# Four instead of six deferred tiles in a decoder layer's output projection, with their inputs converted in a fixed order

## The chip, the cores and the metric

The kernel runs on one core of one Trainium2 chip. The metric is the device time of one execution in microseconds (us); three runs of the kernel before gave 1334.19, 1337.36 and 1341.72 us, so the median is 1337.36. The engines are called TensorE (PE in the profile), VectorE (DVE), ScalarE (ACT), GpSimd (POOL) and SyncE (SP), which issues the transfers.

## The reference

One decoder layer is computed for a prompt of 1,024 tokens and for 64 sample tokens (8 sequences of 8), 1,088 tokens in all, with 1,024 features each:

```python
h = rms_norm(x, norm_mix_g)
proj = h @ w_in
a_val, a_gate, q, k, v = jnp.split(proj, [...], axis=-1)
...
a = jax.nn.silu(layer_norm(depthwise_conv_valid(a_full, conv_a_w, conv_a_b), ln_a_g, ln_a_b))
o = attend(q, k, v).reshape(B, S, D_ATTN)
x = x + jnp.concatenate([a, o], axis=-1) @ w_out
h = rms_norm(x, norm_ffn_g)
g_full = jnp.concatenate([ffn_past, h @ w_ffn_gate], axis=1)
g = depthwise_conv_valid(g_full, ffn_conv_w, ffn_conv_b)
x = x + (jax.nn.silu(g) * (h @ w_ffn_up)) @ w_ffn_down
```

The outputs are the normed result, the new keys and values, and the convolutions' states. What the change touches is the product with `w_out`, the residual sum, the norm behind it, and the first tiles of the products with `w_ffn_gate` and `w_ffn_up`.

## The kernel before

Features lie on the 128 partitions and tokens along the free dimension, so `x` is eight tiles of 128 x 1,088. Every fp32 operand of a product is split into a high and a low part (`hi = copy of x` on ScalarE, rounded; `lo = x - hi` on GpSimd or VectorE), and each product is three matmuls: high by high, high by low and low by high.

The product with `w_out` runs over eight feature tiles of the concatenated branch outputs, which are written to DRAM (`mixed`) and read back. It is cut by these input tiles into parts of 3, 3 and 2 (`PARTS`). The first two parts are done by `out_part` (line 855), for each of the eight output tiles in turn: load the weights into a staging buffer (tag WR, two of them), split them into two tiles of tag W (five of them), multiply, and add into `x2[m]`. These products are written so that they fill TensorE while the last heads of attention wait for other engines. The second part (input tiles 3 to 5) is done over all 1,088 tokens only for the output tiles that aren't deferred, in pieces of 384, 384 and 320 tokens (`CHUNKS`). For the deferred ones, `ORDER[:DEFER]`, it is done over the first 544 tokens only, in two pieces of 272 (`HALF`); the rest is left for later.

The last part (input tiles 6 and 7, which attention finishes last) is done by `out_half` (line 1090), once for the first 544 tokens (`out_half(0, ...)`) and once for the others (`out_half(1, ...)`), over the output tiles in the order 4, 5, 6, 7, 0, 1, 2, 3. For each output tile: the products, 12 matmuls of 272 columns in each half; in the second half for a deferred tile 18 more of the second part ahead of them; an addition into the residual on VectorE (L1102), a store of it to DRAM (L1103), a square on ScalarE (L1105), and an addition to the sum of squares on VectorE (L1109). `out_half(1)` also holds the first half's norm: a hook behind output tile j = 1 takes the root (`root`: ten small matmuls at L208, some small steps on VectorE, L210 to L223, and a square root on ScalarE), a hook behind j = 2 spreads it over the partitions (`spread`: transposes at L235 and a copy at L237).

Ahead of `out_half` the inputs are made ready: the last part's inputs (loaded at L975, high parts at L977, low parts at L978 on VectorE) and weights (loads at L983, parts at L988 and L989); the second halves of the three inputs that the deferred products use (L1000 to L1004); their weights, two output tiles to a staging buffer (L1007 to L1014); then four blocks of the first gate weights, `gate0`, and of the first up weights, `up0` (loads at L1035; conversions at L1041, L1042, L1053, L1054; all low parts on GpSimd). None of these conversions is tied to a place in its engine's queue.

Behind `out_half(1)` the first half's normed tiles are scaled and split (`first_blocks`: scaling at L1115, high parts at L1021, low parts at L1022) into the blocks b11 and b21, and `first_half(gate0)` multiplies them. Between its two products stands `between()`, the second half's root; behind the second step of its second product the root is spread. Then the second half's tiles are scaled and split into b22, t1, t3, t2 and t4, and `first_half(up0)` and two `second_half` calls follow. From then on the FFN runs over pairs of feature tiles, `ffn_pair(j)`, which load further weights through the same two staging buffers.

The program's framework sets the order of each engine's queue: it simulates a timeline and takes, of what is ready in it, what comes first in program order. `tc.issue_after(ins)` places what is traced under it behind `ins` in the queue of the engine that `ins` runs on, without a semaphore; instructions of other engines aren't bound by it. On the chip each engine then takes its queue in that fixed order.

## Time and profile before

| what | value |
|---|---|
| median of 3 runs | 1337.36 us (1334.19 to 1341.72) |
| the profiled execution's own time | 1339.12 us |
| its span | 1337.3 us |
| TensorE busy | 1294.3 us, 97% |
| VectorE, ScalarE, GpSimd busy | 930.6, 563.5 and 494.4 us |
| mean granted TensorE clock | 0.988 |

The span is the time from the first to the last record of the profiled execution; its own time, measured from outside, is 1.8 us more. Times inside the span are counted from its start. The stretch that the change edits lies between about 505 us (the last part of attention) and 665 us (the first pair of the FFN). A line of the view of waits says which engine and line waited, for what, for how long in all, how often and the longest time. A line of a timeline gives the start, the duration, the engine and line, the operation with its tiles and shapes, and in brackets the idle time before it with what ended it; rows that follow each other closely are merged (`x2`). Matmuls overlap in their pipeline, so the pace is read from one start to the next, not from a duration.

### The profile page before, as it was taken

Reading aid. Unit: us, or ns where it says so; the run is one execution under the profiler, and the core shown is the slowest. Engines: PE = TensorE matmul, PEld = TensorE weight load, DVE = VectorE, ACT = ScalarE, POOL = GpSimd, SP = SyncE. Lnnn points to the kernel's source line nnn. Section 1 sums busy time; section 2 is a strip of 40 time slices with the busy share of each in tenths; the row PEclk is TensorE's granted clock in tenths of the full one; section 3 lists DMA queues with packets and bytes.
Section 4 is the critical chain, followed back from the end, with each engine's and each line's share of the span. In section 5 each row is a group of like instructions: output and inputs, shape, how many; then the busy total and the mean of one; then the engine's idle time right before and its main releaser. Section 6 shows DMA issues by size and latency. Waiting matters only on the chain.

```text
span 1337.3 us, 26024 instructions
## 1 busy us (share of the span) xinstructions
PE 1294.3 (97%) x10329; PEld 1252.8 (94%) x10329; DVE 930.6 (70%) x1779; ACT 563.5 (42%) x1132; POOL 494.4 (37%) x400
## 2 busy tenths in 40 slices
PE   7999999999999998999999999999999999999996
PEld 7999998999978887889999999999999999999996
DVE  6369779656674656577977677676776659967656
ACT  6412221456674567354534233333333345334432
POOL 1211112111101111870757556464555534444610
PEclk8999999999998999999999999999999999999998
DMA  8147767555779878661023231332313395352412
GB/s 310 56 131 286 281 234 194 181 177 159 219 235 256 218 249 263 201 235 43 14 109 121 92 123 44 111 122 91 119 36 121 101 353 194 108 186 85 156 40 95
DMA packets 94010, 212.30 MB, mean 159 GB/s; under 512 B 13888, under 2 KB 43584, under 8 KB 93888
## 3 DMA queue, kind: packets, MB, share of 16 engines
q1 hardware_dynamic: 93888, 210.64, 48.1%
q8 instruction: 81, 1.33, 0.4%
q14 instruction: 41, 0.34, 0.1%
HBM read 154.56 MB, written 56.04 MB: 157 GB/s over the span
## 4 chain that ended last, share of the span: by engine, by line
PE 81%; DVE 9%; DMA 6%; issue 2%; ACT 1%; POOL 1%; SPq 1%; DVEq 0%; POOLq 0%; ACTq 0%
PE g L186 6%; PE g L188 6%; PE g L187 6%; PE py L925 4%; PE py L927 4%; PE py L928 4%; PE g L925 4%; PE g L928 4%; PE g L927 4%; PE pz L927 3%; PE pz L928 3%; PE pz L925 3%; PE o L746 3%; PE px L925 3%; PE px L928 3%; PE px L927 3%
## 5 line engine op out<-in xcount | busy, mean ns | idle before, releaser
L162 POOL TENSOR_TENSOR wl<-wr,wh 128x1024 fp32r<-128x1024 f32 (+1 forms) x36 | 67.0, 1861 | 278.8 <-PE g L188 152.1
L186 PE MATMUL g<-xh,wh 128*128 128x384 f32 (+1 forms) x472 | 157.5, 334 | 2.5 <-DVE qkv L449 1.4
L188 PE MATMUL g<-xh,wl 128*128 128x384 f32 (+1 forms) x472 | 155.9, 331 | 0.0
L187 PE MATMUL g<-xl,wh 128*128 128x384 f32 (+1 forms) x472 | 155.8, 330 | 0.0
L925 PE MATMUL g<-ux,as 128*128 128x272 f32 x504 | 145.1, 288 | 0.4 <-DVE x L1499 0.4
L928 PE MATMUL g<-ux,as 128*128 128x272 f32 x504 | 145.3, 288 | 0.0
L927 PE MATMUL g<-ux,as 128*128 128x272 f32 x504 | 144.7, 287 | 0.0
L1054 POOL TENSOR_TENSOR wb<-wr,wb 128x512 fp32r<-128x512 f32 x84 | 121.5, 1457 | 51.1 <-ACT wb L1053 51.1
L1409 POOL TENSOR_TENSOR as<-ar,as 128x640 fp32r<-128x640 f32 (+1 forms) x56 | 89.2, 1602 | 104.3 <-ACT as L1408 92.5
L1053 ACT ACTIVATE wb<-wr 128x512 fp32r<-128x512 f32 x84 | 52.5, 628 | 165.4 <-DVE wr L1070 105.1
L925 PEld LDWEIGHTS g<-ux,as 128*128 128x128 f32 x504 | 95.0, 189 | 0.8 <-issue 0.6
L928 PEld LDWEIGHTS g<-ux,as 128*128 128x128 f32 x504 | 94.8, 188 | 0.0
L927 PEld LDWEIGHTS g<-ux,as 128*128 128x128 f32 x504 | 94.7, 188 | 0.0
L186 PEld LDWEIGHTS g<-xh,wh 128*128 128x128 f32 x472 | 89.3, 189 | 4.9 <-issue 2.4
L1279 DVE SCALAR_TENSOR_TENSOR fc<-gb,prm,fc 128x1104 f32<-128x1104 f32 x44 | 82.5, 1893 | 14.7 <-ACT fc L1277 14.4
L698 ACT ACTIVATE y<-y,m 128x128 f32<-128x128 f32 (+1 forms) x192 | 88.5, 464 | 7.4 <-DVE m L686 7.2
L187 PEld LDWEIGHTS g<-xl,wh 128*128 128x128 f32 x472 | 89.3, 189 | 0.1
L188 PEld LDWEIGHTS g<-xh,wl 128*128 128x128 f32 x472 | 89.3, 189 | 0.1
L1054 POOL TENSOR_TENSOR wa<-wr,wa 128x512 fp32r<-128x512 f32 x42 | 58.1, 1386 | 78.2 <-ACT wa L1053 74.2
L160 ACT ACTIVATE wh<-wr 128x1024 fp32r<-128x1024 f32 (+1 forms) x36 | 29.5, 820 | 134.4 <-PE g L188 104.2
L399 DVE SCALAR_TENSOR_TENSOR cacc<-gp,prm,cacc 128x1024 f32<-128x1024 f32 x60 | 84.3, 1405 | 0.1
L661 DVE CUSTOM_DVE_ANT_0 y<-s,pmk 128x128 f32<-128x128 f32 (+1 forms) x192 | 63.8, 377 | 28.0 <-PE s L657 25.4
(381 smaller groups left out, 4315.2 us busy)
## 6 DMA issues: line engine op xcount, KB each, us to landing
cr<-in_kc SPq DMA_DIRECT2D x24, 768.0 KB, 7.8
cr<-in_vc SPq DMA_DIRECT2D x24, 768.0 KB, 7.8
ux<-ub SPq DMA_DIRECT2D x63, 272.0 KB, 4.1
kk<-dk SPq DMA_DIRECT2D x48, 256.0 KB, 5.6
wr<-in_w_gate SPq DMA_DIRECT2D x22, 512.0 KB, 3.3
wr<-in_w_up SPq DMA_DIRECT2D x22, 512.0 KB, 4.6
wr<-in_w_in SPq DMA_DIRECT2D x20, 512.0 KB, 4.8
ub<-u SPq DMA_DIRECT2D x18, 544.0 KB, 3.9
```

The source lines that it names most:

```text
L162: lo_eng.tensor_sub(lo, raw, hi.bitcast(F32))
L186: nc.tensor.matmul(ps[c], whi[:, k, :], xh[:, t0:t0 + n], start=(k == 0), stop=False)
L187: nc.tensor.matmul(ps[c], whi[:, k, :], xl[:, t0:t0 + n], start=False, stop=False)
L188: nc.tensor.matmul(ps[c], wlo[:, k, :], xh[:, t0:t0 + n], start=False, stop=(k == nk - 1))
L399: eng.scalar_tensor_tensor(acc[:, :S], gp[:, j:j + S], col(w0 + j), acc[:, :S], op0=ALU.mult, op1=ALU.add)
L698: nc.scalar.activation(y, y, AF.Exp, bias=m[:, 4 * g + i:4 * g + i + 1], scale=-1.0, accum_out=den[:, g, 2 * hd + u, i:i + 1])
L925: nc.tensor.matmul(ps, whi[:, k, :], xh[:, t], start=(start and k == 0), stop=False, skip_group_check=True)
L927: nc.tensor.matmul(ps, whi[:, k, :], xl[:, t], start=False, stop=False, skip_group_check=True)
L928: nc.tensor.matmul(ps, wlo[:, k, :], xh[:, t], start=False, stop=(stop and k == nk - 1), skip_group_check=True)
L1054: nc.gpsimd.tensor_sub(lo, x, hi.bitcast(F32))
L1279: nc.vector.scalar_tensor_tensor(c[:, :W], gb[i][:, t:t + W], col(C_FW + 3 * f + t), c[:, :W], op0=ALU.mult, op1=ALU.add)
L1409: nc.gpsimd.tensor_sub(lo, raw, hi.bitcast(F32))
```

## The change

`DEFER` goes from 6 to 4: the output tiles 0 and 1 do the second part over all tokens in `out_part`. The loads for the deferred products are chained, each behind the one before on SyncE's queue and all behind the last part's inputs; the three inputs now come ahead of the weights. Their conversions are put in a list of seven (three inputs, four tiles' weights), and `out_half(0)`'s hook issues one of them behind each of the squares j = 1 to 7 on ScalarE; the low parts stay on GpSimd. `gate0`'s loads and conversions and `up0`'s loads are traced behind `out_half(0)` instead of ahead of it. `up0`'s conversions are traced in `between()`, and its low parts go from GpSimd to VectorE, behind the last step of the second half's root.

```diff
@@ -60,7 +60,7 @@
...
-ORDER, DEFER = (4, 5, 6, 7, 0, 1, 2, 3), 6
+ORDER, DEFER = (4, 5, 6, 7, 0, 1, 2, 3), 4
...
@@ -960,7 +960,6 @@
         sft = zt("F", "sft", 1, "sft", NF * B * 2).rearrange("p (j b t) -> p j b t", b=B, t=2)
         early = {"gate": [zt("F", "WA", 2, "wa", D, F32R) for _ in range(2)],
                  "shared": [zt("F", "tmp", 4, "ta", HN) for _ in range(2)],
-                 "wd": [slot("t4", "wh", w=384) for _ in range(4)],
                  "up": [slot("t4", "wa", w=D // 2) for _ in range(4)], "rb": [slot("t3", "rb", F32)],
                  "b21": [slot("b21", "wh", w=512)], "t2": [slot("t2", "mh")], "b11": []}
 
@@ -994,24 +993,40 @@
 
         n1 = PARTS[-2]
         kd = k0 - n1
-        deferred, wd = [], {}
-        for i in range(n1):
-            raw = slot("t2", "mx", F32)
-            nc.sync.dma_start(raw, mixed[kd + i][:, HN:])
+        deferred, wd, later = [], {}, []
+
+        def later_input(raw):
             hi, lo = slot("t3", "mh"), slot("t3", "ml")
             nc.scalar.activation(hi, raw, AF.Copy)
             nc.gpsimd.tensor_sub(lo, raw, hi.bitcast(F32))
             deferred.append((hi, lo))
+
+        def later_weight(m, raw):
+            hi, lo = [slot("b22", t, w=n1 * P) for t in ("wh", "wl")]
+            nc.scalar.activation(hi, raw, AF.Copy)
+            nc.gpsimd.tensor_sub(lo, raw, hi.bitcast(F32))
+            wd[m] = [t.rearrange("p (k c) -> p k c", c=P) for t in (hi, lo)]
+
+        def load_later(dst, src):
+            nonlocal last_load
+            with tc.issue_after(last_load):
+                last_load = nc.sync.dma_start(dst, src).ins
+
+        for i in range(n1):
+            raw = slot("t2", "mx", F32)
+            load_later(raw, mixed[kd + i][:, HN:])
+            later.append((later_input, raw))
         for m0 in ORDER[:DEFER:2]:
             raw = wp.tile([P, D], F32, tag="WR", name=nm("wr"), bufs=WR)[:, :2 * n1 * P]
-            last_load = nc.sync.dma_start(raw.rearrange("p (m c) -> p m c", m=2),
-                                          w_out[m0:m0 + 2, :, kd * P:k0 * P].rearrange("m p c -> p m c")).ins
+            load_later(raw.rearrange("p (m c) -> p m c", m=2),
+                       w_out[m0:m0 + 2, :, kd * P:k0 * P].rearrange("m p c -> p m c"))
             for i in range(2):
-                r = raw[:, i * n1 * P:(i + 1) * n1 * P]
-                hi, lo = [slot("b22", t, w=n1 * P) if len(wd) < 4 else early["wd"].pop(0) for t in ("wh", "wl")]
-                nc.scalar.activation(hi, r, AF.Copy)
-                nc.gpsimd.tensor_sub(lo, r, hi.bitcast(F32))
-                wd[m0 + i] = [t.rearrange("p (k c) -> p k c", c=P) for t in (hi, lo)]
+                later.append((later_weight, m0 + i, raw[:, i * n1 * P:(i + 1) * n1 * P]))
+
+        def convert(j, square):
+            for call, *args in later[j - 1:j] if j else ():
+                with tc.issue_after(square):
+                    call(*args)
...
@@ -1035,15 +1050,15 @@
...
-        def weight_parts(x, new):
+        def weight_parts(x, new, eng):
             n = x.shape[-1]
             hi, lo = new
             nc.scalar.activation(hi, x, AF.Copy)
-            nc.gpsimd.tensor_sub(lo, x, hi.bitcast(F32))
+            eng.tensor_sub(lo, x, hi.bitcast(F32))
             hi, lo = [t.rearrange("p (k c) -> p k c", c=P) for t in (hi, lo)]
             return [(hi[:, i:i + 4], lo[:, i:i + 4]) for i in range(0, n // P, 4)]
 
-        def block_tile(x, zone=False):
+        def block_tile(x, zone=False, eng=nc.gpsimd):
 
             if zone:
                 t = early["gate"].pop(0) if early["gate"] else zt("F", "WA", 2, "wa", D, F32R)
@@ -1051,7 +1066,7 @@
                 t = wp.tile([P, D], F32R, tag="W", name=nm("wb"))
             hi, lo = t[:, :half], t[:, half:]
             nc.scalar.activation(hi, x, AF.Copy)
-            nc.gpsimd.tensor_sub(lo, x, hi.bitcast(F32))
+            eng.tensor_sub(lo, x, hi.bitcast(F32))
...
@@ -1077,12 +1092,6 @@
...
-        gate0 = plain_blocks(weight_raw(w_gate, 0))
-        raw = weight_raw(w_up, 0)
-        up0 = []
-        for i in range(2):
-            up0 += weight_parts(raw[0][:, i * half:i * half + half], early["up"][2 * i:2 * i + 2])
-        up0 += [block_tile(raw[1][:, i * half:i * half + half]) for i in range(2)]
...
@@ -1102,12 +1111,12 @@
                 residuals.append(nc.vector.tensor_add(x, all_of(ps), x).ins)
                 nc.sync.dma_start(x2d[m][:, c], x)
                 s = slot("t1", "sq", F32)
-                nc.scalar.activation(s, x, AF.Square)
+                square = nc.scalar.activation(s, x, AF.Square).ins
                 if j == 0:
                     acc = s
                 else:
                     nc.vector.tensor_add(acc, s, acc)
-                hook(j)
+                hook(j, square)
...
@@ -1117,10 +1126,10 @@
         def new_root(s):
             return early["rb"].pop() if early["rb"] else slot("t3", s, F32)
 
-        sq0, _ = out_half(0, lambda m: None)
+        sq0, _ = out_half(0, convert)
         rs = []
 
-        def norm_first(j):
+        def norm_first(j, square):
             if j == 1:
                 rs.append(root(sq0, D, HN))
             elif j == 2:
@@ -1132,6 +1141,8 @@
                     scale(0, i, rs[0])
                 split(x2[i][:, :HN], tag, i - k)
 
+        gate0 = plain_blocks(weight_raw(w_gate, 0))
+        raw, up0 = weight_raw(w_up, 0), []
         sq1, residuals = out_half(1, norm_first)
         quads = [(*halves(x2[k]), *halves(x2[k + 4])) for k in range(4)]
 
@@ -1159,6 +1170,11 @@
 
         def between():
             rs.append(root(sq1, D, HN))
+            with tc.issue_after(rooted[0]):
+                for i in range(2):
+                    up0.extend(weight_parts(raw[0][:, i * half:i * half + half], early["up"][2 * i:2 * i + 2],
+                                            nc.vector))
+                up0.extend(block_tile(raw[1][:, i * half:i * half + half], eng=nc.vector) for i in range(2))
 
         def spread_second(k, last):
             if k == 1:
```

## The prediction

> **What bounds the kernel now.** I began with the page's head and busy times.
>
> ```profile
> span 1337.3 us, 26024 instructions
> ...
> PE 1294.3 (97%) x10329; PEld 1252.8 (94%) x10329; DVE 930.6 (70%) x1779; ACT 563.5 (42%) x1132; POOL 494.4 (37%) x400
> ```
>
> TensorE is busy 97% of the span; only what delays TensorE, or lets its clock fall, costs time. The view of what TensorE waited for lists few waits, and three of the longer ones lie in the stretch that the change edits: the start of the first half's output products (L977), the first deferred products (L1003) and the first half's norm (the memset L210 stands in VectorE's queue right behind the root's last step, L223).
>
> ```profile
> PE g L925 <- ACT mh L977: 3.2, 1, 3.2
> ...
> PE g L235 <- DVE rv L210: 1.5, 1, 1.5
> ...
> PE g L927 <- POOL ml L1003: 1.2, 3, 0.8
> ...
> PE py L925 <- DVE gb L1260: 0.8, 1, 0.8
> ```
>
> To price them I cut that stretch into windows. The columns are the window, its length, TensorE's busy time with its matmuls in brackets, then the other engines; after POOL stand the granted clock and the DMA share.
>
> ```profile
> 561.30:568.60 7.30, 4.05 (x20) 3.65 (x19) 3.26 (x3) 3.83 (x8) 5.87 (x5) 0.77 0.75 270
> 568.60:578.64 10.04, 10.04 (x83) 10.04 (x81) 6.71 (x10) 6.15 (x12) 7.07 (x7) 1.00 0.73 256
> 578.64:585.30 6.66, 5.06 (x24) 4.09 (x23) 6.56 (x8) 5.05 (x10) 6.66 (x5) 0.75 0.89 345
> ...
> 594.95:596.70 1.75, 0.28 (x3) 0.09 (x2) 1.72 (x4) 0.00 (x0) 1.58 (x2) 1.00 0.88 306
> 596.70:611.80 15.10, 15.10 (x119) 14.89 (x120) 14.22 (x22) 7.18 (x12) 0.00 (x0) 1.00 0.28 97
> ```
>
> ```profile
> 567.27 0.43 PE L928 MATMUL g<-mh,wl 128*128 128x272 f32 x1
> 567.50 0.43 PE L927 MATMUL g<-ml,wh 128*128 128x272 f32 x1
> ...
> 568.72 0.29 PE L928 MATMUL g<-mh,wl 128*128 128x272 f32 x1
> 568.85 0.29 PE L925 MATMUL g<-mh,wh 128*128 128x272 f32 x1
> ```
>
> Starts in the timeline of TensorE give the pace: 0.125 us from one 272-column matmul to the next at full clock (568.72 to 568.85), 0.23 at the lower one (567.27 to 567.50). At full clock, 20 matmuls are 2.5 us, so the first window loses 4.8 of its 7.30 us; the third has 24, or 3.0 us, and loses 3.7 of 6.66; the fourth is 1.75 us in which TensorE has almost nothing, a loss of 1.6. The second, between them, is full, and so is the last, in which VectorE is nearly full too. I call the losses A (4.8), B (3.7) and C (1.6): 10.1 us, the pool from which this change can draw. Two of them hold a slower clock, 0.77 and 0.75, as well as idle time.
>
> **Why they are there.** SyncE's queue, GpSimd and ScalarE:
>
> ```profile
> 556.00 0.33 SPq L766 DMA_DIRECT2D mixed<-cat  x1
> 556.44 2.84 SPq L983 DMA_DIRECT2D wr<-in_w_out  x2
> 559.33 0.50 SPq L975 DMA_DIRECT2D mx<-mixed  x1
> ...
> 567.07 3.97 SPq L1007 DMA_DIRECT2D wr<-in_w_out  x2
> 571.14 1.37 SPq L1000 DMA_DIRECT2D mx<-mixed  x3
> ...
> 594.06 0.33 SPq L1035 DMA_DIRECT2D wr<-in_w_gate  x1
> ```
>
> ```profile
> 557.86 1.01 POOL L162 TENSOR_TENSOR wl<-wr,wh 128x384 fp32r<-128x384 f32 x1 [1.54 <-ACT wh L160]
> ...
> 575.60 2.49 POOL L1013 TENSOR_TENSOR wh<-wr,wh 128x384 fp32r<-128x384 f32 x2 [2.27 <-ACT wh L1012]
> 578.05 5.41 POOL L1003 TENSOR_TENSOR ml<-mx,mh 128x544 fp32r<-128x544 f32 x3
> ...
> 591.01 3.02 POOL L1042 TENSOR_TENSOR wa<-wr,wa 128x512 fp32r<-128x512 f32 x2 [1.11 <-ACT wa L1041]
> 594.02 2.51 POOL L1054 TENSOR_TENSOR wb<-wr,wb 128x512 fp32r<-128x512 f32 x2
> ```
>
> ```profile
> 574.99 0.53 ACT L1012 ACTIVATE wh<-wr 128x384 fp32r<-128x384 f32 x1 [2.78 <-DMA wr<-in_w_out]
> 575.42 0.64 ACT L1105 ACTIVATE sq<-x 128x544 f32<-128x544 f32 x1
> ...
> 643.33 0.64 ACT L1053 ACTIVATE wa<-wr 128x512 fp32r<-128x512 f32 x1 [0.79 <-issue]
> ```
>
> A is latency: attention's last output is stored at 556.00 (L766), the last products' inputs are requested at 559.33 (L975), and the output products that fill TensorE meanwhile run out at 561.3. B is order: the deferred inputs are requested last (L1000, 571.14), behind weight loads (L1007) that wait for staging buffers, and GpSimd makes their low parts (L1003, from 578.05 to 583.5) behind the sixth tile's weights (L1013, 575.60). ScalarE sits 2.78 us at 574.99 on such a weight load, with squares queued behind it.
>
> **The change, part by part.** *Four tiles, not six.* Two tiles' second halves go from out_half(1) back to out_part: 2 x 18 matmuls x 0.125 = 4.5 us of TensorE, only moved (the tile's 1,088 columns, now in three pieces, are the same work). In out_part they lie ahead of A, and so fill it: its end goes from 561.3 to about 565.8. The inputs' first high parts ended the wait 3.2 us after 561.3, at about 564.6, so the gap could close. Two things can undo that. Weight tiles come from five buffers, two to a tile, so the low part of the last weights (L162, 557.86) must then wait for products that end up to 4.5 us later; the two L983 loads wait for staging that this frees, and L975 stood behind them. And attention's own steps may be held up by the added filler. Bounds: 0 (the gap moves along) to 4.8 (gone). I take 3.3, leaving about 0.5 us of idle and 1.0 of slow clock, because L975 comes first in program order and is free to pass a delayed L983.
>
> A rule of the Trainium skill (page TensorE: Matmul & The Clock Gate, Part 1) says that the clock drops after at least one idle window of about 3.4 us. Loss B disagrees: its longest single wait is 0.8 us, and yet the clock was 0.75. By the rule the short gap left in A would cost no slow clock and the sum below would be 7.9, not 6.9; I go by the row.
>
> *The bound order.* The loads become L975, then the three deferred inputs, then two weight loads, each issued after the one before; the seven conversions go one behind each of the squares 1 to 7 of out_half(0). A wait is added on ScalarE: behind a conversion whose load is late stand the later squares, then VectorE's sums of them (L1109) and the root. Say out_half(0) starts at t. A tile is 12 matmuls, 1.5 us; eviction, square and conversion behind it are 0.71, 0.64 and about 0.65.
>
> ```profile
> 580.38 0.71 DVE L1102 TENSOR_TENSOR x<-g,x 128x544 f32<-128x544 f32 x1
> 581.01 1.23 DVE L1109 TENSOR_TENSOR sq<-sq,sq 128x544 f32<-128x544 f32 x1
> ...
> 592.80 1.25 DVE L221 TENSOR_TENSOR rt<-rr 128x5 f32<-128x5 f32 x1
> ...
> 613.81 2.38 DVE L1109 TENSOR_TENSOR sq<-sq,sq 128x544 f32<-128x544 f32 x3
> 619.00 0.16 DVE L212 TENSOR_SCALAR rv<-g 128x4 f32<-128x4 f32 x1 [2.81 <-PE g L208]
> ...
> 619.71 0.17 DVE L221 TENSOR_TENSOR rt<-rr 128x5 f32<-128x5 f32 x1 [0.28 <-ACT rr L218]
> ...
> 624.37 5.66 DVE L1115 SCALAR_TENSOR_TENSOR x<-x,prm,rb 128x544 f32<-128x544 f32 x8 [4.08 <-ACT rb L237]
> ...
> 652.32 0.68 DVE L1068 TENSOR_TENSOR s<-wr 128x512 f32<-128x512 f32 x1
> ```
>
> (0.71 and 1.23 in the first two rows are the eviction L1102 and a sum L1109 while GpSimd runs.) The first input's high part is ready at t + 3.0 + 2.1 = t + 5.1. GpSimd's three low parts at 1.8 each (5.41 for the three of L1003) end at t + 10.6, the first weights' (1.0 to 1.5, from the 2.49 and 2.51 for pairs of L1013) at t + 11.9; the first deferred product is due at t + 12.0, the second weights 3.8 us after that (30 matmuls). It just fits. With sums at 1.23, VectorE takes 1.9 us a tile instead of 1.5 and the chain slips by about half a us. Bounds for what goes of B: 1.0 (the chain slips by 2 us and the clock falls again) to 3.7. I take 3.0.
>
> *Two weight pairs fewer; gate and up weights later.* GpSimd loses L1013's last pair, 2.5 us, and up0's four low parts (L1042 and L1054 from 591.01, 5.5 us). The four of gate0 stay, behind the deferred weights: staging frees at about t + 13.5 and 15.5, a load takes some 3.3 us (3.34 in the chain of waits, for the same size), so they end near t + 23, long before first_half wants them.
>
> ```profile
> 586.94 3.34 DMA wr<-in_w_up
> ```
>
> The root's three steps took 1.25 us each beside up0's GpSimd work and 0.17 with GpSimd idle (L221 at 592.80 and 619.71). After the change the first root starts near t + 20, beside gate0's conversions instead of up0's. Bounds for C: -0.5 to 1.6; I take 0.6, since gate0 still covers most of it.
>
> *up0's low parts on VectorE.* Four subtractions of 128x512 behind the second root, 0.68 each (L1068, the same size, at 652.32): 2.7 us. They land where VectorE sits 4.08 us waiting for the spread root (before 624.37). ScalarE's four high parts aren't bound to that and go into idle time. The loads of pair 1's gate weights (L1035 at 594.06 and after), which wait for the same two staging buffers, move behind those subtractions, some 25 us later; their first conversion (L1053) is only at 643.33, so about 20 us of slack covers it, and a us beyond that would cost a us.
>
> *Less cover.* From the first spread to the first gate products TensorE had 15.1 us of work (the window from 596.70) and will have 10.6. VectorE must in that time scale and split b11 and b21, and finish the eight sums for the second root.
>
> ```profile
> 617.86 1.10 PE L208 MATMUL g<-ones,sq 128*128 128x1 f32 x10
> ```
>
> The sums end at 616.2 (613.81 + 2.38), 1.7 us ahead of the root's matmuls at 617.86. With 4.5 us less in between, TensorE would wait 2.8 us if VectorE kept its order. But sums and evictions are traced ahead of the splits and come ready sooner, and a b21 split isn't needed until a us after the root, the last one 4.5 us later still. In all VectorE gets 4.5 + 2.7 = 7.2 us tighter against idle time of 2.81 + 4.08 = 6.9. Bounds: 0 to 2.8 lost at the root, up to 7.2 if none of that idle time can be used; I take 0.
>
> Sum: 3.3 + 3.0 + 0.6 - 0 = 6.9 us. The profiled execution took 1339.1 us for a span of 1337.3; it becomes 1332.2 (span 1330.4). It lies 1.8 above the median of 1337.4, so the median becomes 1330.5, 0.52% less. All that follows is bound by TensorE and should just start earlier. Half a per cent is about what a measurement of this kernel can tell from no change: 6.7 us, so below 1330.7 is faster and above 1344.1 slower.
>
> **The rivals.** *The gap moves instead of closing.* The five weight buffers hold back L983 and with it L975, or the filler delays attention's last steps, so A stays whole and only B and C pay: 3.6 us, 1333.8. For it: no row shows slack in that chain; the last L162 ends at 558.9 and L983's second load and L975 follow at once. Against: program order puts L975 first.
>
> *VectorE becomes the bound behind out_half(1).* If its two idle stretches are waits that move along with TensorE, they take up nothing: the 7.2 us reappear on TensorE at the second root and at the b22 products, with 1.6 us of slow clock after such a gap (A's 4.8 less the wait of 3.2). That is 8.8 against 6.9 saved: 1.9 slower, 1339.3. It decides from the point where the sums end after TensorE has reached the root. For it: VectorE is 14.22 us busy in the 15.10 us after 596.70, and TensorE already waits 0.8 us for it at L1260. Against: the idle 4.08 is right where the subtractions are put.
>
> *All three losses go whole*, GpSimd being done before the root starts: 10.1 us, 1327.3.
>
> **How the numbers follow.** The forecast has 0.55, two thirds of it below the bound (its centre lies 0.2 below, and A can pay more): 0.37 faster, 0.18 the same. The moved gap 0.20 (0.18 the same, 0.02 slower, should attention's end suffer more than the gap). VectorE as the bound 0.13 (0.08 the same, 0.05 slower, where the slow clock lasts). All three losses whole 0.12, faster. Faster 0.49, same 0.44, slower 0.07. The forecast's own range is 1327.5 to 1334; for eight in ten I go from 1326 (the whole pool and a us of scatter) to 1337.5 (half of the VectorE case left out).
>
> **What would show it.** Right: the window between out_part's end and out_half(0) has less than 1.5 us without matmuls; the wait for L1003's successor on GpSimd is gone and the clock stays at 1.00 there; DMA requests for deferred inputs come before 568; the four subtractions stand on VectorE between the second root and L1115 without a wait of TensorE behind them; first_half starts about 7 us earlier than 611.8. Wrong: TensorE idles as long as before ahead of out_half(0) (the moved gap), waits at the second root or for b22 (VectorE), or ScalarE's conversions hold squares back for a late load.

## The result and the profile after

The changed kernel takes 1345.57 us (median of 9 runs, 1341.79 to 1349.71) against 1336.41 (9 runs, 1333.16 to 1341.72) of the kernel before: a ratio of 1.0067 (95% interval 1.0047 to 1.0086), 9 us slower. The prediction was 1330.5. The profiled execution of the changed kernel took 1341.79, the lowest of its runs.

```profile
span 1340.1 us, 25967 instructions
...
PE 1294.4 (97%) x10311; PEld 1251.1 (93%) x10311; DVE 936.2 (70%) x1785; ACT 561.6 (42%) x1130; POOL 486.6 (36%) x394
```

TensorE's busy time is what it was (1294.3), so no work was added. The span is only 2.8 us longer because attention happened to run shorter: its last product (L746) starts at 542.6 instead of 548.3. (The stretch ahead of it scatters: from the first L657 to the last L746 it took 320.0 us here and 326.4 in e4_gps, a kernel below that is the same up to there.) From that product to the last matmul the changed execution takes 8.1 us more, 789.4 instead of 781.3, which agrees with the medians.

The same kind of windows as in the prediction, now over the changed kernel (window, length, TensorE's busy time with matmuls in brackets, PEld, DVE, ACT, POOL, granted clock, DMA share, GB/s):

```profile
560.08:566.35 6.27, 4.08 (x20) 3.64 (x19) 3.00 (x3) 3.78 (x6) 4.33 (x4) 0.73 0.55 198
...
576.30:583.50 7.20, 5.04 (x24) 4.43 (x23) 4.87 (x5) 3.41 (x7) 7.17 (x6) 0.76 0.94 345
583.50:593.18 9.68, 9.68 (x80) 9.65 (x80) 4.77 (x10) 3.55 (x7) 5.49 (x4) 1.00 0.52 181
593.18:603.76 10.58, 10.58 (x85) 10.37 (x84) 9.46 (x15) 7.30 (x13) 0.00 (x0) 1.00 0.35 129
...
616.30:621.10 4.80, 3.34 (x28) 3.06 (x27) 3.24 (x12) 2.33 (x6) 0.00 (x0) 1.00 0.01 2
```

At 0.125 us a matmul, A (the first row, 20 matmuls) loses 6.27 - 2.5 = 3.8 us; it was 4.8. B (the second, 24) loses 7.20 - 3.0 = 4.2; it was 3.7. C is gone: the third and fourth rows, on both sides of the first root's spread at 593.18, are full. So 1.0 - 0.5 + 1.6 = 2.1 us were saved, of 6.9 foreseen. And there is a new loss in the last row, where TensorE is busy 3.34 of 4.80 us. What TensorE waited for from 540 to 700 us:

```profile
PE py L928 <- POOL wb L1069: 1.8, 1, 1.8
PE g L925 <- ACT mh L976: 1.7, 1, 1.7
PE g L235 <- DVE rr L223: 1.5, 1, 1.5
PE g L925 <- ACT wh L1006: 1.3, 2, 0.9
PE g L928 <- POOL wl L1007: 0.9, 1, 0.9
```

The second, fourth and fifth rows are A and B. The third is the new wait at the second root's spread; the first is one at the second FFN pair, `ffn_pair(1)`, whose gate products take 19.3 us there and took 16.1 before: 3.2 us more. The last new loss lies much later, where the products with `w_ffn_down` begin (L925 with `ux`, behind the last up product `pz`). TensorE's timeline, and VectorE's for the instruction that it waits for:

```profile
1080.73 0.28 PE L928 MATMUL pz<-t4h,wb 128*128 128x272 f32 x1
1084.41 0.36 PE L925 MATMUL g<-ux,as 128*128 128x272 f32 x1 [3.40 <-DVE u L1314]
```

```profile
1083.55 0.72 DVE L1314 TENSOR_TENSOR u<-pz,u 128x544 f32<-128x544 f32 x1
```

The kernel before has no wait there (`pz` at 1083.53 and `g` at 1083.65). With the slow clock behind it (granted 0.61 from 1084.41 to 1088.00, where it was 1.00 in the kernel before), the stretch from the last block's first up product (`px`) to the first of the layer's closing products is 5.2 us longer: 1060.6 to 1276.3, before 1063.4 to 1273.9.

SyncE's queue shows why A and B stayed:

```profile
551.24 0.33 SPq L766 DMA_DIRECT2D mixed<-cat  x1
...
554.78 2.63 SPq L982 DMA_DIRECT2D wr<-in_w_out  x2
557.46 0.50 SPq L974 DMA_DIRECT2D mx<-mixed  x1
...
568.23 0.32 SPq L1112 DMA_DIRECT2D x2d<-x  x1
568.65 1.67 SPq L1013 DMA_DIRECT2D mx<-mixed  x3
570.42 0.90 SPq L1013 DMA_DIRECT2D wr<-in_w_out  x2
```

Attention's last store is at 551.24, but the inputs (L974) still stand behind the weight loads (L982), which wait for staging (2.63 us issued as a pair from 554.78). So L974 comes 6.2 us behind that store, where L975 came 3.3 us behind it (559.33 against 556.00): 2.9 of the 4.5 us that the filler adds are lost again. And the first residual store (L1112) stands ahead of the deferred loads (L1013). It waits for VectorE until 568.23, and the loads with it: they come 6.6 and 8.4 us behind the projection's first product (562.07), where it was 6.3 for the inputs (571.14 against 564.82), while of the weights the first load came 1.1 us ahead of it (563.76) and the other two from 2.3 us behind it. So a conversion bound behind a square has nothing to convert yet: ScalarE waits 2.0 us for a weight load at 576.75.

VectorE around the second root:

```profile
594.59 1.48 DVE L1124 SCALAR_TENSOR_TENSOR x<-x,prm,rb 128x544 f32<-128x544 f32 x2 [0.49 <-ACT rb L237]
...
612.16 0.72 DVE L1118 TENSOR_TENSOR sq<-sq,sq 128x544 f32<-128x544 f32 x1
617.49 0.16 DVE L212 TENSOR_SCALAR rv<-g 128x4 f32<-128x4 f32 x1 [4.61 <-PE g L208]
...
618.68 0.69 DVE L1057 TENSOR_TENSOR wa<-wr,wa 128x512 fp32r<-128x512 f32 x1
...
621.10 5.66 DVE L1124 SCALAR_TENSOR_TENSOR x<-x,prm,rb 128x544 f32<-128x544 f32 x8
```

From its first scaling (594.59) to its last sum (612.88) VectorE works for 18.3 us almost without a gap; in the kernel before it is 18.1 (598.08 to 616.19). TensorE, however, starts the products with b11 9.2 us after that first scaling, where it was 13.7, since two tiles' deferred products are gone from `out_half(1)`. It would reach the second root 3 us ahead of the sums (it is done with b11 at 609.9), and the framework put the root behind the products with b21 instead. There the sums wait for it (4.61 us of idle VectorE), and its latency, which b21 used to hide, lies open. From the first product with b11 to the second pair TensorE takes 52.1 us (603.76 to 655.90), where it took 50.1 (611.81 to 661.92): this costs 2.0 us.

### The profile page after: what moved, and what is told of

It is laid out like the page before. It is cut to its first block, busy times and chain, and to the rows that moved or that the text cites. A ratio compares the mean times of both kernels' runs of the same rounds, so it can differ in the third digit from the quotient of the medians.

```text
span 1340.1 us, 25967 instructions
## 1 busy us (share of the span) xinstructions
PE 1294.4 (97%) x10311; PEld 1251.1 (93%) x10311; DVE 936.2 (70%) x1785; ACT 561.6 (42%) x1130; POOL 486.6 (36%) x394
## 4 chain that ended last, share of the span: by engine, by line
PE 81%; DVE 9%; DMA 5%; ACT 2%; issue 1%; POOL 1%; SPq 1%; DVEq 0%; POOLq 0%; ACTq 0%
PE g L186 6%; PE g L187 6%; PE g L188 6%; PE py L928 5%; PE py L927 5%; PE py L925 4%; PE g L925 4%; PE g L928 4%; PE g L927 4%; PE px L925 3%; PE pz L925 3%; PE pz L927 3%; PE pz L928 3%; PE px L928 3%; PE px L927 3%; PE s L657 3%
## 5 line engine op out<-in xcount | busy, mean ns | idle before, releaser
L925 PE MATMUL g<-ux,as 128*128 128x272 f32 x504 | 145.8, 289 | 3.8 <-DVE u L1314 3.4
L1069 POOL TENSOR_TENSOR wb<-wr,wb 128x512 fp32r<-128x512 f32 x82 | 120.1, 1475 | 55.4 <-ACT wb L1068 55.4
L1069 POOL TENSOR_TENSOR wa<-wr,wa 128x512 fp32r<-128x512 f32 x42 | 65.4, 1560 | 126.6 <-ACT wa L1068 124.6
L925 PEld LDWEIGHTS g<-ux,as 128*128 128x128 f32 x504 | 95.7, 190 | 4.4 <-issue 4.4
```

The source lines that it names most:

```text
L925: nc.tensor.matmul(ps, whi[:, k, :], xh[:, t], start=(start and k == 0), stop=False, skip_group_check=True)
L1069: eng.tensor_sub(lo, x, hi.bitcast(F32))
```

## The experiments

Theories: **P**, two buffers of PSUM, the memory that the matmuls add into, coincide at the last products; **S/I**, SyncE's order keeps A and B; **R/M**, with four tiles VectorE's 18 us from the first root to the second root's sums have too little TensorE work beside them. The rival throughout is **V**: the four subtractions given to VectorE are the cost. Every kernel was timed in turn with the kernel before, the e, f, g and h kernels on different chips, so ratios are compared and not medians. The intervals are about 0.18% to each side, so two kernels can be told apart when they differ by about 0.25%.

| kernel | tiles | median us | ratio to before | 95% interval |
|---|---|---|---|---|
| changed | 4 | 1345.57 | 1.0067 | 1.0047 to 1.0086 |
| e1_bank | 4 | 1341.00 | 1.0043 | 1.0025 to 1.0060 |
| e2_store | 4 | 1337.22 | 1.0007 | 0.9990 to 1.0024 |
| e3_inputs | 4 | 1336.39 | 1.0000 | 0.9986 to 1.0014 |
| e4_gps | 4 | 1342.36 | 1.0041 | 1.0022 to 1.0061 |
| f3_number | 4 | 1337.71 | 1.0023 | 1.0005 to 1.0041 |
| f1_first_root | 4 | 1335.65 | 1.0001 | 0.9981 to 1.0022 |
| f5_both_roots | 4 | 1336.71 | 1.0010 | 0.9990 to 1.0030 |
| g3_scale_free | 4 | 1335.24 | 0.9988 | 0.9968 to 1.0008 |
| f4_six | 6 | 1333.04 | 0.9979 | 0.9960 to 0.9999 |
| h2_only_six | 6 | 1334.58 | 0.9985 | 0.9968 to 1.0002 |
| g1_six_gps | 6 | 1339.87 | 1.0025 | 1.0007 to 1.0043 |
| h1_six_late | 6 | 1336.63 | 1.0001 | 0.9981 to 1.0020 |
| g2_up_only | 6 | 1337.37 | 1.0009 | 0.9987 to 1.0030 |
| g4_six_inputs | 6 | 1336.04 | 1.0007 | 0.9987 to 1.0027 |

**e1_bank.** TensorE's wait ends with L1314, the addition that reads the last `pz`. Theory P: in the changed kernel that `pz` and the first chain of the last products got the same of the four pair buffers, in the kernel before different ones; they are dealt out in the order in which the framework schedules, which the change shifted. The edit takes one buffer more (`turn` is set for the last pair of up products only):

```diff
...
+            if turn:
+                nc.tensor.matmul(pair("turn")[:1, :1], ones, ones, start=True, stop=True)
             block_product(z, s3, blocks["t3"], True)
...
```

> The changed kernel with one 1x1 matmul into a pair buffer of its own ahead of the last up product z (behind it the four pair buffers are dealt out one place further), so that the last product of the second half and the first chain of the last products no longer share a buffer. Theory P (a pair buffer costs 3.4 us of waiting and 1.7 of slow clock at the start of the last products): the wait of the first of them for the combination of u disappears, and the kernel is 4 to 5.5 us faster than the changed one, about 1341, 0.3% above the kernel before. Rival V (the loss is VectorE's, whose conversions and late second root push everything behind them): the wait only turns into one for the weights or the sums right behind, gain 0 to 1.5 us, about 1344 to 1345.5.

```profile
1082.88 0.28 PE L928 MATMUL pz<-t4h,wb 128*128 128x272 f32 x1
1083.00 0.30 PE L925 MATMUL g<-ux,as 128*128 128x272 f32 x1
```

The wait is gone (0.12 us from `pz` to `g`), as P says; the same stretch takes 211.2 us, where it was 215.7 in the changed kernel and 210.5 before. The trace gives 4.5 us; the times give 0.24% or 3 us, at the edge of what they can tell.

**e2_store and e3_inputs.** Both start from e1_bank.

```diff
-                nc.sync.dma_start(x2d[m][:, c], x)
+                with tc.issue_after(last_load):
+                    nc.sync.dma_start(x2d[m][:, c], x)
```

> As e1_bank, and the residual stores of the output projection bound behind the last deferred load, so that SyncE no longer stands at the first store (until 568.2 us in the changed kernel) with the deferred loads behind it. Theory S (the loss at the start of the second half's output projection, 3.7 us, stayed because the store stood ahead of the loads): the loads are issued at about 560 to 562 us instead of 568 to 570, the waits of TensorE for the converted deferred weights (0.85, 0.44, 0.86 us) and the slow clock behind them go, and the kernel is 3 to 4 us faster than e1_bank. Rival (the conversions are bound to the squares, and these come no sooner): the deferred parts are converted one behind each square whenever the loads land, so the last of them stays where it was; gain under 1 us.

```profile
566.10 1.51 SPq L1013 DMA_DIRECT2D mx<-mixed  x3
567.71 3.31 SPq L1013 DMA_DIRECT2D wr<-in_w_out  x2
574.28 6.57 SPq L1113 DMA_DIRECT2D x2d<-x  x6
```

The deferred loads now stand right behind the inputs and ahead of the first store, and the kernel gains 0.36%, 4.8 us, more than the 3 to 4 expected. In the trace 2.8 us of it lie between the first half's first product and the first root (23.2 instead of 26.0 us): that is B, against 25.4 in the kernel before. Another 3.4 lie at the second FFN pair, whose gate products take 16.0 instead of 19.4, while 1.5 are lost in between, 1.0 of it at a slow clock behind the second root (granted 0.78 from 622.90 to 630.52).

What made the second pair's weights late shows in the traces, first of the changed kernel, then of e2_store:

```profile
658.91 3.23 POOL L1069 TENSOR_TENSOR wb<-wr,wb 128x512 fp32r<-128x512 f32 x1 [6.10 <-ACT wb L1068]
```

```profile
660.93 0.71 DVE L1341 TENSOR_TENSOR u<-pz,ta 128x544 f32<-128x544 f32 x1
```

```profile
663.65 1.30 POOL L1069 TENSOR_TENSOR wb<-wr,wb 128x512 fp32r<-128x512 f32 x1 [7.00 <-ACT wb L1068]
```

The low part that TensorE waits for (L1069) took GpSimd 3.23 us, in e1_bank too, and 1.30 in e2_store. In the first case VectorE worked beside it with inputs in SBUF only, until L1341, which reads PSUM; GpSimd ended 1.2 us after that one began. The last section has more of this. There was no slack for it: L1069 starts as TensorE comes to these products (py at 658.92), where in the kernel before it started 6.9 us ahead of them (658.02 against 664.93). The pair's first weights had long been loaded (from 620.65); these conversions stand later in the queues.

```diff
-            nc.sync.dma_start(raw.rearrange("p (m c) -> p m c", m=4),
-                              w_out[m0:m0 + 4, :, k0 * P:].rearrange("m p c -> p m c"))
+            with tc.issue_after(last_load):
+                nc.sync.dma_start(raw.rearrange("p (m c) -> p m c", m=4),
+                                  w_out[m0:m0 + 4, :, k0 * P:].rearrange("m p c -> p m c"))
```

> As e1_bank, and the first half's weight loads for the output projection bound behind the last deferred input, so that the four inputs of the first half go ahead of them on SyncE; the deferred loads then also stand ahead of the first residual store. Theory I (the loss ahead of the output projection comes from the weight loads that wait for a weight buffer with the inputs behind them on SyncE): the four inputs are issued at about 551 to 555 us, the wait of the first half's output projection for its inputs (1.7 + 0.5 us) goes, and with the deferred loads early too the kernel is 4 to 6 us faster than e1_bank. Rival G (the gap only moves): the projection then waits as long for its weights, which are issued later, and only the part of the deferred loads is gained, 0 to 3 us, or it is lost again.

(The edit binds the two weight loads behind the last of the last part's four inputs; the deferred loads follow.) e3_inputs is as fast as e2_store. With the inputs first, TensorE still waits 1.8 us ahead of the projection, now for the weights (1.7 in e2_store, for the inputs): rival G for A, while B goes as in e2_store.

**e4_gps**, from e1_bank:

```diff
-                                            nc.vector))
-                up0.extend(block_tile(raw[1][:, i * half:i * half + half], eng=nc.vector) for i in range(2))
+                                            nc.gpsimd))
+                up0.extend(block_tile(raw[1][:, i * half:i * half + half]) for i in range(2))
```

> As e1_bank, and the four low parts of the first up weights subtracted on GpSimd again, at the same place (behind the second half's root). Theory V (VectorE bound): the second half's scale, which starts 17.3 us behind the first products in the changed kernel and 12.6 in the kernel before, starts 2.5 us earlier (four subtractions of 0.60 to 0.69 us less), and the kernel is 2 to 4 us faster than e1_bank. Rival R (the second root itself is put late, behind the products with b21, and the subtractions then only fill the wait): the scale starts no more than 1 us earlier, GpSimd, which needed 9.5 us for one conversion in that stretch, becomes later, and the kernel is the same as or slower than e1_bank by up to 3 us.

No difference from e1_bank (1.0041 and 1.0043). But the place wasn't the same, as the expectation had it: the binding is to an instruction of VectorE and doesn't hold GpSimd's queue. GpSimd made these low parts from 599 to 605.5 us, ahead of the second root. In the trace two things cancel: from b11 to the second pair TensorE takes 57.0 us (52.1 in e1_bank), at the second pair's gate products 16.1 (19.4). So e4_gps alone doesn't settle V; f4_six and g1_six_gps do, below.

**The number of tiles: f3_number and f4_six.** The kernel before with only the number changed (and e1_bank's matmul), and e1_bank with the number changed back:

```diff
-ORDER, DEFER = (4, 5, 6, 7, 0, 1, 2, 3), 6
+ORDER, DEFER = (4, 5, 6, 7, 0, 1, 2, 3), 4
```

> The kernel before with four deferred tiles in place of six and nothing else of the change (and the matmul into a pair buffer of its own, as in e1_bank, so that the start of the last products is free of the buffer wait). Theory R (with four tiles the second half's projection is 36 matmuls or 4.5 us shorter, VectorE's work from the first root to the second root's sums still takes 19.5 us, so the second root's matmuls stand behind the products with b21 and its latency lies open): the second root follows b21 as in the changed kernel, TensorE waits 1.0 to 1.5 us ahead of the spread, and the kernel takes 1338 to 1341, slower than before by 0.2 to 0.4%. Rival B (what costs is the bound order of the conversions): the number alone does not hurt, 1333 to 1336.

```diff
-ORDER, DEFER = (4, 5, 6, 7, 0, 1, 2, 3), 4
+ORDER, DEFER = (4, 5, 6, 7, 0, 1, 2, 3), 6
...
-            for call, *args in later[j - 1:j] if j else ():
+            for call, *args in (later[j - 1:j] if j < KT - 1 else later[j - 1:]) if j else ():
```

> e1_bank with six deferred tiles again: the conversions bound behind the squares (the last two weight parts together with the seventh behind the last square), the first up weights on VectorE. Theory R: the second root's matmuls stand ahead of b21 again, the 1.5 us wait ahead of the spread and the late scale go; 2 to 4 us faster than e1_bank, 1337 to 1339 (the wait at the start of the second half's projection stays, and may grow as the conversions come later). Rival B (the bound order costs): slower than e1_bank, 1341 to 1345.

f3_number is slower than before by 0.23%, 3 us, as R has it (its median a little below the range given). Its second root stands behind b21 (613.46; b21 from 607.51), TensorE waits 0.8 us at the spread, and behind it the granted clock is 0.78 (617.00 to 624.38): from b11 to the second pair it takes 53.2 us, 3.0 more than before. f4_six gains 0.64% on e1_bank, 8.6 us, over twice what was expected, and is faster than the kernel before by about 0.2%. Its windows and VectorE (its lines stand one below those of the changed kernel):

```profile
557.39:563.50 6.11, 3.12 (x18) 2.68 (x17) 3.94 (x4) 3.90 (x7) 5.13 (x4) 0.88 1.02 378
...
574.97:577.00 2.03, 1.71 (x14) 1.49 (x13) 2.03 (x4) 1.30 (x3) 2.03 (x3) 1.00 0.39 152
...
587.45:603.00 15.55, 15.39 (x123) 14.99 (x121) 13.99 (x22) 9.49 (x17) 3.03 (x2) 1.00 0.38 135
```

```profile
590.00 2.56 DVE L1125 SCALAR_TENSOR_TENSOR x<-x,prm,rb 128x544 f32<-128x544 f32 x2 [1.50 <-ACT rb L237]
...
606.81 2.38 DVE L1119 TENSOR_TENSOR sq<-sq,sq 128x544 f32<-128x544 f32 x3
610.95 0.16 DVE L212 TENSOR_SCALAR rv<-g 128x4 f32<-128x4 f32 x1 [1.77 <-PE g L208]
...
612.15 0.68 DVE L1058 TENSOR_TENSOR wa<-wr,wa 128x512 fp32r<-128x512 f32 x1
...
616.33 5.66 DVE L1125 SCALAR_TENSOR_TENSOR x<-x,prm,rb 128x544 f32<-128x544 f32 x8 [1.68 <-ACT rb L237]
```

With six tiles the framework itself puts the deferred loads ahead of the first store, and B shrinks to 0.3 us (14 matmuls, 1.75 of 2.03). The window behind the first spread is 15.5 us and nearly full, 123 matmuls. The sums end at 609.19 and the root follows b11 at 609.82. VectorE's four subtractions (from 612.15) fall into its wait for the spread, as the prediction wanted. A keeps 3.9 us (18 matmuls, 2.25 of 6.11): two tiles less fill it. V as the cause of the loss has fallen with this kernel: VectorE makes the four subtractions, and the loss is gone.

**h2_only_six** is the changed kernel with the number alone put back.

> The changed kernel with six deferred tiles and nothing else of f4_six (no matmul into a buffer of its own: with six tiles the last product of the second half and the first chain of the last products come to lie in different pair buffers by themselves). Theory N (the number is what made the change a loss, by the order of the loads, of the second root and of the pair buffers that follows from it): as f4_six, 1331 to 1335, faster than the kernel before by 0.1 to 0.4%. Rival (f4_six was a lucky run, or its extra matmul matters): 1336 to 1340.

It gives 0.9985, so the number is worth 0.82%, 11 us, within the change. Without the added matmul its last products start without a wait. Its gain on the kernel before, 0.15%, has an interval that reaches no change.

**What the cover is worth with four tiles: f1_first_root, f5_both_roots, g3_scale_free**, each on top of the one before, from e2_store:

```diff
-            if j == 1:
+            if j == 0:
                 rs.append(root(sq0, D, HN))
-            elif j == 2:
+            elif j == 1:
```

> e2_store with the first half's root and its spread asked for one tile earlier in the second half's projection (30 matmuls or 3.8 us sooner in TensorE's order; the sums of the first half stood ready 6.7 us ahead of the root in the changed kernel). Theory R (the second root's place, behind b21, sets the loss): VectorE's sums for the second root are ready 3.8 us sooner, but the root's matmuls stay behind b21, so the gain is under 1 us: 1336 to 1338. Rival V (VectorE is the bound from the first root on, and all behind it moves with it): 3 to 4 us faster than e2_store, 1333 to 1334.

```diff
             between()
-            two_products(o, (a12, a22), blocks["b21"], False, hook)
+            with tc.issue_after(summed[0]):
+                two_products(o, (a12, a22), blocks["b21"], False, hook)
```

> f1_first_root, and the products with b21 bound behind the second root's matmuls, so that the root follows the products with b11 as in the kernel before. Theory R: the sums are ready as TensorE has done b11 (about 15.5 us behind the start of the first root's spread), the root waits under 1 us, its latency lies beside b21, VectorE's conversions of the first up weights fall into the 4 us that VectorE waits for the spread; 2.5 to 4 us faster than e2_store, 1333 to 1335, 0.05 to 0.2% below the kernel before. Rival V (VectorE's sums come no sooner than 19.5 us behind the spread): TensorE waits 2 to 3.6 us for the root at once and then again at a slow clock, no gain or up to 2 us of loss, 1337 to 1339.

```diff
-                with tc.issue_after(made[-2] if len(made) > 1 else residuals[2]):
+                with tc.issue_after(made[-2] if len(made) > 1 else residuals[0]):
```

> f5_both_roots (four tiles), and the first scale bound behind the first residual sum of the second half and not the third, as VectorE stood idle from the spread to the third sum there (593.2 us against a spread at 587.8). Theory M (with four tiles 36 matmuls, 4.5 us, moved from beside VectorE's 18 us of scaling, splitting and summing to where TensorE is the bound; what remains of the loss is that VectorE begins too late): VectorE's chain starts 2 to 4 us sooner, the wait for the second root (3.0 us) goes to under 1 us, and the kernel is 2 to 4 us faster than f5_both_roots, 1332.5 to 1334.5, as fast as f4_six. Rival W (the sums cannot come sooner, as they follow the last tiles of the projection): under 1 us, 1336 to 1337.

The wait for the second root's sums, first of f5_both_roots, then of g3_scale_free:

```profile
PE g L208 <- DVE sq L1119: 3.0, 1, 3.0
```

```profile
PE g L208 <- DVE sq L1119: 0.9, 1, 0.9
```

f1_first_root gained nothing that can be measured (0.06%), as theory R has it. In f5_both_roots the root is back ahead of b21, and TensorE waits 3.0 us for the sums: R's hope for them was wrong, and its rival V right about the wait, because the first scaling, bound behind the third residual of the second half, starts only at 599.17, 5.4 us behind the spread. Unbound from it, in g3_scale_free, it starts 1.4 us behind the spread (590.15 against 588.77), and the wait goes to 0.9 us; the times, 0.22% below f5_both_roots and 0.19% below e2_store, are inside what they can tell. By the traces the three edits only take back what the second of them cost: from b11 to the second pair TensorE takes 53.1 us in e2_store, 53.7, 56.4 and 53.5 in these three, and 50.1 in the kernel before. Behind the 0.9 us in g3_scale_free the granted clock is still 0.70 (612.05 to 617.69). So with the store bound and the buffers apart the loss of the change is gone with four tiles too (1.0007 and 0.9988), but the lost cover keeps costing about 3 us there, and no kernel with four tiles is shown to be faster than six.

**Which engine, and where: g1_six_gps, g2_up_only, h1_six_late.** g1_six_gps is f4_six with e4_gps's edit; g2_up_only is the kernel before (and e1_bank's matmul) with the change's edits of `between()` and of `up0` alone; h1_six_late holds GpSimd's own queue:

> f4_six with the low parts of the first up weights on GpSimd again, so that of the change only the bound order of the conversions (and the first up weights' place behind the second root) is left. Theory O (the order is what gained 2.8 us against the kernel before, VectorE only fills 4 us in which it waits): 1332.5 to 1335. Rival U (the gain is VectorE's, GpSimd being late with the up weights in the kernel before): 1335.5 to 1338, no better than the kernel before.

> The kernel before with six deferred tiles and its conversions in their old order, of the change only the first up weights: low parts on VectorE behind the second root. Theory O (the order is the gain): 1334.5 to 1337, as the kernel before; the losses at the start of the second half's projection stay. Rival U: 1332 to 1334.

```diff
-            with tc.issue_after(rooted[0]):
+            mark = nc.gpsimd.tensor_copy(sp.tile([P, 9], F32, tag="mark", name=nm("mark"), bufs=1)[:, :1],
+                                         rs[-1][:, :1]).ins
+            with tc.issue_after(mark):
```

> f4_six with the low parts of the first up weights on GpSimd, but really behind the second half's root: one small GpSimd copy of the root stands ahead of them, and they are bound behind it (in e4_gps and g1_six_gps the binding was to an instruction of VectorE, which does not hold GpSimd's queue; there they ran ahead of the root, beside VectorE's sums, whose instructions took 1.81 us instead of 0.71 to 0.78). Theory K (GpSimd's subtractions slow VectorE's by 1.1 us each while they run, and g1_six_gps lost its 6 us because that fell into VectorE's chain ahead of the second root): VectorE's sums are back to 0.7 us each and the waits of 3.5 and 0.9 us at the first products are gone, 1333 to 1336; some of it is paid behind the root, where VectorE scales beside them. Rival U (the up weights must be VectorE's, GpSimd is simply late with them): the first products with the up weights wait for them by 2 to 5 us, 1337 to 1341.

g1_six_gps is 0.46% slower than f4_six: theory O fell, and not by GpSimd being late, as its rival had it. VectorE and GpSimd of g1_six_gps, and what TensorE then waits for:

```profile
592.27 1.81 DVE L1119 TENSOR_TENSOR sq<-sq,sq 128x544 f32<-128x544 f32 x1
...
597.77 0.71 DVE L1112 TENSOR_TENSOR x<-g,x 128x544 f32<-128x544 f32 x1
598.40 1.28 DVE L1038 TENSOR_TENSOR b11l<-x,b11h 128x544 fp32r<-128x544 f32 x1
599.60 1.81 DVE L1125 SCALAR_TENSOR_TENSOR x<-x,prm,rb 128x544 f32<-128x544 f32 x1
```

```profile
591.73 3.50 POOL L1058 TENSOR_TENSOR wa<-wr,wa 128x512 fp32r<-128x512 f32 x2
597.80 3.03 POOL L1070 TENSOR_TENSOR wb<-wr,wb 128x512 fp32r<-128x512 f32 x2 [2.57 <-ACT wb L1069]
```

```profile
PE py L943 <- DVE x L1112: 3.5, 1, 3.5
```

Sums (L1119), splits (L1038) and scalings (L1125) that take 0.71 to 0.78 us elsewhere take up to 1.81 beside GpSimd's subtractions; the residual addition (L1112) at 597.77 starts with one of them and takes 0.71. VectorE falls behind, and TensorE waits 3.5 us for a residual addition: `py` takes the PSUM buffer that the addition reads. In h1_six_late the same subtractions run behind the root:

```profile
594.10 0.71 DVE L1119 TENSOR_TENSOR sq<-sq,sq 128x544 f32<-128x544 f32 x1
```

```profile
590.56 3.04 POOL L1070 TENSOR_TENSOR wb<-wr,wb 128x512 fp32r<-128x512 f32 x2 [1.28 <-ACT wb L1069]
...
614.02 1.28 POOL L1058 TENSOR_TENSOR wa<-wr,wa 128x512 fp32r<-128x512 f32 x1
```

The sums are at 0.71 again as soon as the gate weights' low parts (590.56, until 593.6) are done, and the 3.5 us wait is down to 0.2. It gains 0.24% on g1_six_gps and stays 0.22% behind f4_six. Both lie just under what the times can tell; the mechanism is in the traces. The Trainium skill (SBUF — State Buffer, Who interferes with whom) says that a VectorE instruction with two inputs in SBUF contends with a GpSimd instruction that reads SBUF, and that one with at most one SBUF input, outside VectorE's two-port modes, doesn't. The traces agree: 1.81 us for the former, 0.71 for L1112, whose other input is in PSUM. g2_up_only doesn't differ from the kernel before (1.0009): moving `up0` alone, without the order, brings nothing that can be measured.

**g4_six_inputs** is f4_six with e3_inputs's edit.

> f4_six with the first half's weight loads bound behind the last deferred load, so that the four inputs are issued first, as in e3_inputs. Theory I (the 2.4 + 0.6 us wait ahead of the projection is for inputs that stand behind weight loads on SyncE): 2 to 3.5 us faster than f4_six, 1329.5 to 1331. Rival G (the gap moves, now the weights are late, as in e3_inputs): within 1 us of f4_six or slower, 1332.5 to 1335.

```profile
PE g L235 <- DVE rv L210: 4.9, 1, 4.9
PE g L925 <- ACT wh L989: 4.5, 1, 4.5
```

It is 0.28% slower than f4_six. Ahead of the projection TensorE now waits 4.5 us, and for the weights, where f4_six waits 2.3 for the inputs: G, the gap moves. (At the first root's spread it waits 4.9 us besides, as the root's square root stands on ScalarE behind a conversion that waits 3.0 us for its gate weights; the two aren't told apart in the time.) A needs inputs and weights at the same time, and neither order gives both; a third staging buffer wasn't tried.

## Why the prediction was wrong

The sum failed at two of its own terms above all, B and *Less cover*, and at two losses for which it had no term.

- **A, taken at 3.3 us: 1.0.** The filler lies where it should, but L974 did not pass L982 and came 2.9 us later behind attention's last store. The step "free to pass a delayed L983" failed, and the rival "the gap moves", which had 0.20, is close to what came; e3_inputs and g4_six_inputs show that the other order moves the gap too.
- **B, taken at 3.0: -0.5.** The step that failed is "the loads become L975, then the three deferred inputs": I read the order in which the loads are traced and took it for SyncE's queue. The residual store, which nothing bound, went between them. With the store bound (e2_store), 2.8 us of the changed kernel's 4.2 go, which leaves 1.4 where it was 3.7 before: the mechanism was right, and worth 2.3.
- **C, taken at 0.6: 1.6.** The bound "up to 1.6" was reached: only the first of the root's three steps still ran beside `gate0`'s low parts (1.24 us, the others 0.17), and TensorE had products until the spread. The text expected `gate0` to cover most of the root; that its low parts ended at 592.57, just ahead of the second step at 592.63, was not worked out there, so this hit is luck.
- **Less cover, taken at 0: 2.0.** The text had 2.8 us of wait at the root as the bound "if VectorE kept its order", and excused it by earlier sums and a later b21. This step failed: VectorE's 18 us didn't shorten, and the framework answered by putting the root behind b21, with 1.5 us of wait at the spread. The number alone (f3_number) costs 3.0 us there. So the rival "VectorE becomes the bound" had the place and the condition right, sums that end after TensorE could have reached the root, but not the size: its 8.8 us contained 2.7 for the four subtractions, which weren't the cost (f4_six has them and gains), and no wait came at the b22 products.
- **Not foreseen: 3.2 us at the second pair's gate products.** The text's 20 us of slack were for the pair's first conversion, and its loads were indeed in time. A later conversion, a low part on GpSimd, was held up beside VectorE (3.23 us for 1.30) at a place where nothing was left to spare.
- **Not foreseen: 5.2 us at the last products**, some 460 us behind the edit. "All that follows is bound by TensorE and should just start earlier" left out that a changed schedule deals out the PSUM buffers anew.

By the trace the sum is 2.1 saved, and 2.0, 3.2 and 5.2 lost: 8.3 us slower, where the medians say 9. What stays open: why the framework puts the store ahead of the loads with four tiles and behind them with six (argued only: its simulated timeline has the loads' memory free at another time), and why it puts the second pair's conversions so late.

## What to carry to other kernels

Before work is moved out of a stretch, ask what that work was hiding there: taking 4.5 us of matmuls from beside an 18 us chain on VectorE cost 2.0 us of TensorE in the changed kernel and 3.0 in f3_number. A queue's order is read from the program that the framework made, not from the order of the source; every instruction that isn't bound (here a store) can land between two that are, and an order bound on one engine doesn't hold another. After any change of schedule, look through the whole profile for new waits, not only at the edit; a buffer dealt out differently cost 5.2 us, where the whole change was meant to bring 6.9. Here the bound order and the VectorE low parts together look worth keeping with six tiles (0.9979 and 0.9985 in two kernels, the second not told from no change by itself); the number wasn't.

## What the runs showed of the hardware

GpSimd can be held up far longer than it holds up VectorE. In the changed kernel one subtraction of 128x512 took 9.58 us, and the next of the same form 1.29:

```profile
638.03 9.58 POOL L1069 TENSOR_TENSOR wa<-wr,wa 128x512 fp32r<-128x512 f32 x1 [45.46 <-ACT wa L1068]
...
648.37 1.29 POOL L1069 TENSOR_TENSOR wa<-wr,wa 128x512 fp32r<-128x512 f32 x1
```

VectorE in that stretch went through thirteen instructions with all inputs in SBUF without a gap, and then came to the first with an input in PSUM:

```profile
646.37 0.65 DVE L1278 TENSOR_TENSOR gb<-pv,ta 128x480 f32<-128x480 f32 x1
```

GpSimd ended 1.24 us after that one began (638.03 + 9.58 - 646.37). So it seems to have stood through all thirteen, and then to have run at its usual pace. The 3.23 us at the second pair fit this: GpSimd ended 1.21 us after L1341 began (658.91 + 3.23 - 660.93). The Trainium skill (SBUF — State Buffer, Summary: rules for kernel authors) says of such a pair that the second one to issue blocks fully until the first finishes; here GpSimd was held up for longer than one VectorE instruction.

The clock fell behind short waits again, as in the prediction's B: the longest single wait in the changed kernel's B is 0.9 us (2.2 in all) and the window's clock 0.76, where the Trainium skill (TensorE: Matmul & The Clock Gate, Part 1) asks for an idle window of about 3.4 us.
